# The sample's attention: from beside the output projection to between the steps of the prompt's attention

## Chip, core and metric

The kernel runs on one core of a Trainium2 chip. The metric is device time in microseconds (us) of one execution; less is better.

## What is computed

One inference step of a decoder layer, for a prompt of 2048 tokens and a sample group of 8 sequences with 8 new tokens each (64 tokens) over a cache of 2048 keys and values. The layer is h = x + W_o [A(n) | B(n)], y = h + W2 relu(RMSNorm(h) W1)^2, with n = RMSNorm(x), D = 1024. A is softmax attention, 8 heads of 64, over three strided key sets merged by their denominators; B is an RWKV-7 time mix. Cut to what matters here:

```
for w, d in ((128, 1), (512, 4), (2048, 16)):       # window, dilation
    s = q @ k[last w, every d].T * scale + bias     # masked to the band
    mx = max(s); e = exp(s - mx); dn = sum(e); o = e @ v
att = sum_b exp(mx_b - max mx) * o_b / sum_b exp(mx_b - max mx) * dn_b
h = x + concat(att, rwkv) @ w_out
```

It is evaluated once for the prompt (no cache) and once for the sample (keys and values from the cache and the 8 new ones).

## The kernel before

Everything is fp32; the large products are done with a high and a low part in three passes. The program is written tile by tile; a planner fixes the order of the instructions on every engine at compile time, by program order as priority and its own estimate of readiness. On the chip each engine, and SP's queue that issues nearly all transfers, goes through its list strictly in order.

**Stage 1** (until about 1208 us of the span): input projections and the RWKV scan. **Stage 2**, the prompt's attention: `attention(p, pump, ahead)` for four head pairs p. For each p it goes through three branches b; a branch has four groups, each with its own values tile `vt`. A step is: scores by two matmuls per block into a bank of `psc` (three banks, two used by a step; lines 1066 and 1067), bias and row minimum on VectorE (L1069), exp on ScalarE, transposes through `ppt` (two banks, L1084) and the product with the values into `ppo` (L1091). A step ends with `pump()`. There are 8 + 8 + 4 = 20 steps per p, 80 in all. `kq_load` fetches the next pair's queries and keys (12 transfers of 512 KB) during branch 1.

`merge(p)` is a generator that merges the three branches. It takes the statistics through a small DRAM tile (`wD`, L1166, back as `wrow`, L1169), then does 12 products (L1176) with a multiply on VectorE each, and stores `mixA` (L1181). `pump` advances the merge of the previous pair by two pieces; the merge of the last pair has nothing left to run beside and uses `psc`, the others `pax` (one bank).

**Stage 3**, the output projection: 8 chunks of 264 columns; for each of 8 output tiles 24 matmuls (L1431) into one of four `pwo` banks, 1536 in all, over panels `mr` of mixA and mixR (L1313) that are split into two parts first.

**The sample's attention** is `sample_attention(b, psa)`, a generator for one of the 8 sequences, with 8 pieces: three of scores (L1233, L1236: keys from the cache in tiles `kv` of 512 KB, L1231), one of exp and sums, three of transposes (L1269) and products with the values (L1277: values in `kv` tiles too, L1264) and one that transposes the result into `attS` (L1282). In the projection two pieces run after each output tile:

```
tt(h[:, o, c0:c0 + NC_], ps[:, :NC_], h[:, o, c0:c0 + NC_], ALU.add)
for _ in range(2):
    next(sample, None)
```

It has its own three PSUM banks (pool `psa`), four `kv` buffers in two pools, and one accumulation over all 11 value blocks. `attS` is needed by the last chunk only. The sample's bias (`sbias`, 32 small loads, L1341 to L1344), its queries and its new keys are loaded after the third pair's attention.

Of the kernel before, what the change touches and what calls it, by code (L numbers as in the profile page):

```python
# [17 lines left out]
P = 128  # L18
# [3 lines left out]
NS = 64  # L22
# [148 lines left out]
def _build(ctx, tc, nc, I, O, dbg, upto):  # L171
# [794 lines left out]
    ae = ph2.enter_context(pool(name="ae", bufs=1))  # L966
    ar = ph2.enter_context(pool(name="ar", bufs=1))

    kqb = ph3.enter_context(pool(name="kqb", bufs=6, side="right"))
# [38 lines left out]
    def bias_load(p, b):  # L1008
        bts = []
        for ty in range(2):  # L1010
            bt = ae.tile([P, 256], F32, name=f"bt{b}{ty}")
            nc.sync.dma_start(out=bt, in_=bass.AP(tensor=bvD.tensor, offset=bvD.offset + (2 * p + ty) * P * 1152 + b * 384 + 127, ap=[[1151, P], [1, 256]]))
            bts.append(bt)
        return bts
# [22 lines left out]
    def attention(p, pump, ahead):  # L1037
# [4 lines left out]
        for b in range(3):  # L1042
# [7 lines left out]
            for grp in range(4):  # L1050
                vp, vt = vt, next_v()
                o = ppo.tile([P, 512], F32, name="o")
                for t2 in range(0, 4, 2 if b < 2 else 4):
# [3 lines left out]
                    for ty in range(2):  # L1057
                        kst, klo, qst = K[ty]
                        ps = psc.tile([P, 512], F32, name="sc")
                        e = ae.tile([P, 512], F32, name="e", bufs=4)  # L1060
                        blocks = []
                        for x, i in enumerate(tl):
                            both = b < 2 and not (i == 0 if b == 0 else i < 4)
                            n = 256 if both else 128
                            c0 = x * w + w - n
                            PE.matmul(ps[:, c0:c0 + n], cols(qst, b, i, False), cols(kst, b, i, both), start=True, stop=False)  # L1066
                            PE.matmul(ps[:, c0:c0 + n], cols(qst, b, i, False), cols(klo, b, i, both), start=False, stop=True)  # L1067
                            nm, dn = st[:, 0, b, i // 4, ty, i % 4:i % 4 + 1], st[:, 1, b, i // 4, ty, i % 4:i % 4 + 1]
                            V.tensor_tensor_reduce(out=e[:, c0:c0 + n], in0=ps[:, c0:c0 + n], in1=bts[ty][:, 256 - n:256], scale=-1.0, scalar=3e38, op0=ALU.add, op1=ALU.min, accum_out=nm)  # L1069
# [33 lines left out]
    def merge(p, ob, st):  # L1103
# [46 lines left out]
        yield  # L1150
        dn = at.tile([P, P], F32, name="dn")
        dm = at.tile([P, P], F32, name="dm")
# [50 lines left out]

    kvs = []

    def kv_tile():

        kv_tile.n += 1
        pl, bufs = kvs[kv_tile.n % len(kvs)]
        return pl.tile([P, 1024], F32, name="kv", bufs=bufs)  # L1210

    kv_tile.n = -1

    def sample_attention(b, psa):
        pr = sat.tile([P, 136 + 520 + 1288], F32, name="pr")
# [11 lines left out]
        for k0, n, parts in runs:  # L1227
            ps = psa.tile([P, 512], F32, name="sc", tag="sp", bufs=2)
            for k1 in range(0, n, 256):
                kt = kv_tile().rearrange("p (q n) -> p q n", q=4)  # L1230
                nc.sync.dma_start(out=kt, in_=I["kc"][b, :, :, k0 + k1:k0 + k1 + 256].rearrange("p q n -> q p n"))  # L1231
                for p in range(4):
                    PE.matmul(ps[32 * p:32 * p + 32, k1:k1 + 256], qbd[:, b, p], kt[:, p], start=True, stop=True, tile_position=(0, 32 * p))  # L1233
            for p in range(4):
                if n == 256:
                    PE.matmul(ps[32 * p:32 * p + 32, 256:264], qbd[:, b, p], kSs[:, p, b * 8:b * 8 + 8], start=True, stop=True, tile_position=(0, 32 * p))  # L1236
            for x, dst, bias, s0, d0, w in parts + (new if n == 256 else ()):
# [13 lines left out]
        yield  # L1251
        o = psa.tile([P, 512], F32, name="ax", tag="ax")

        blocks = [(520 + i * P, P, 4 + i) for i in range(6)] + [(i * P, P, i) for i in range(4)] + [(512, 8, None)]
        for q0 in range(0, 11, 4):
            bl = blocks[q0:q0 + 4]
            vts = []
            for y in range(0, len(bl), 2):
# [6 lines left out]
                vts.append(vt)  # L1265
            pt = psa.tile([P, 512], F32, name="pt", tag="sp", bufs=2)
            pts = sat.tile([P, 512], F32, name="pts", bufs=2)
            for y, (c0, n, kb) in enumerate(bl):
# [3 lines left out]
            else:  # L1272
                V.tensor_copy(pts[:, :2 * P], pt[:, :2 * P])
                V.tensor_copy(pts[:8, 2 * P:3 * P], pt[:8, 2 * P:3 * P])
            for y, (c0, n, kb) in enumerate(bl):
                for p in range(4):
                    PE.matmul(o[32 * p:32 * p + 32, 0:P], pts[:n, y * P + 32 * p:y * P + 32 * p + 32], vts[y // 2][:n, y % 2, p * P:(p + 1) * P], start=(q0 == 0 and y == 0), stop=(kb is None), tile_position=(0, 32 * p))  # L1277
            yield
        os_ = sat.tile([P, P], F32, name="os", tag="pts", bufs=2)
        act(os_, o[:, :P], AF.Copy, scale=rd)  # L1280
        tp = psa.tile([P, 512], F32, name="tp", tag="sp", bufs=2)
        PE.transpose(tp[:, :P], os_, ident)  # L1282
# [4 lines left out]

    def sample_all(psa):
        for b in range(8):
            yield from sample_attention(b, psa)  # L1290

# [26 lines left out]

    rest = iter(())
    for p in range(4):  # L1320
        before = rest
        def pump():
            for _ in range(2):
                next(before, None)

        rest = attention(p, pump, ahead)
        for _ in before:
            pass
        if p == 2:
            kqa.close()  # L1330
            we = ph3.enter_context(pool(name="we", bufs=1, side="right"))
            sat = ph3.enter_context(pool(name="sat", bufs=1, side="right"))

    sbias = sat.tile([P, 136 + 520 + 1288], F32, name="sbias")
    sb1, sb4, sb16 = sbias[:, 0:136], sbias[:, 136:656], sbias[:, 656:]
    G.memset(sbias, 0.0)
    for h in range(8):
        r0 = 32 * (h // 2) + 8 * (h % 2)
        o0 = svD.offset + h * 8 * NSV + 7
        win = lambda b, c, n: bass.AP(tensor=svD.tensor, offset=o0 + b * 528 + c, ap=[[NSV - 1, 8], [1, n]])  # L1340
        nc.sync.dma_start(out=sb1[r0:r0 + 8], in_=win(0, 384, 136))  # L1341
        nc.sync.dma_start(out=sb4[r0:r0 + 8], in_=win(1, 0, 520))
        nc.sync.dma_start(out=sb16[r0:r0 + 8, :520], in_=win(2, 0, 520))
        nc.sync.dma_start(out=sb16[r0:r0 + 8, 520:].rearrange("i (m r) -> i m r", r=8), in_=bass.AP(tensor=svD.tensor, offset=o0 + 3 * 528, ap=[[NSV - 1, 8], [16, 96], [1, 8]]))  # L1344
    qSs = sat.tile([P, 4, NS], F32, name="qSs", tag="pts", bufs=2)
    nc.sync.dma_start(out=qSs, in_=qSD.rearrange("h p t -> p h t"))
    kSs = sat.tile([P, 4, NS], F32, name="kSs")
    nc.sync.dma_start(out=kSs, in_=kSD.rearrange("h p t -> p h t"))
    qbd = sat.tile([P, 8, 4, 32], F32, name="qbd")
    G.memset(qbd, 0.0)  # L1350
    for ty in range(2):
        rr = slice(ty * 64, ty * 64 + 64)
        for p in range(4):
            G.tensor_copy(qbd[rr, :, p, ty * 8:ty * 8 + 8], qSs[rr, p].rearrange("p (b i) -> p b i", i=8))
    attS = sat.tile([P, 4, NS], F32, name="attS")

    kvs.append((sat, 2))
    for k in (4, 5):
        wo_panel(we.tile([P, 2 * D], F32R, name=f"wo{k}"), k)
    mixed = {}  # L1360
    for k in range(4, 8):
        mixed[k, 0] = mix_panel(we, k, 0)
    for _ in rest:
        pass
    ph2.close()
# [42 lines left out]

    with pool(name="wo2", bufs=1) as wo2, pool(name="pwo", bufs=4, space=PSUM, side="right") as pwo, pool(name="psa", bufs=1, space=PSUM) as psa, pool(name="pst", bufs=1, space=PSUM) as pst:
        kvs.append((wo2, 2))  # L1410
        sample = sample_all(psa)
        for k in (6, 7, 0, 1, 2, 3):
# [4 lines left out]
        for c0 in range(0, NT, NC_):  # L1417
            if c0 + NC_ == NT:
                for _ in sample:
                    pass  # L1420
            nc.sync.dma_start(out=h[:, :, c0:c0 + NC_], in_=I["xh"][:, :, c0:c0 + NC_])  # L1421
# [3 lines left out]
            for o in range(KT):  # L1425
# [7 lines left out]
                tt(h[:, o, c0:c0 + NC_], ps[:, :NC_], h[:, o, c0:c0 + NC_], ALU.add)  # L1433
                for _ in range(2):
                    next(sample, None)
            while tile_ < 17 and ends[tile_] <= c0 + NC_ < NT:
# [110 lines left out]
```

## Time and profile before

| | |
|---|---|
| median of 3 runs | 3414.67 us (3407.58 to 3416.85) |
| the profiled execution's own time | 3415.77 us |
| its span | 3414.0 us |
| TensorE (PE) busy | 3209.2 us, 94% |
| PE weight loads (PEld) busy | 2791.4 us, 82% |
| VectorE (DVE) / ScalarE (ACT) / GpSimd (POOL) busy | 1713.4 / 1326.7 / 395.2 us |
| transfers | 364.73 MB, 107 GB/s over the span |

In the view of windows a row is a stretch from A to B us of the span, its length, the busy time of each engine with its instructions in brackets, the mean granted clock of TensorE as a share of 2.4 GHz (PEclk), the busy share of the 16 DMA engines, and GB/s. The chain is followed back from the last instruction; its rows have the start, the length and what ran. In the view of waits a row has who waited, for whom, the sum in us, how often, and the longest. In the timeline a row has the start, the length, the engine (SPq is SP's queue), the line and the instruction. In the view of groups a row has line, engine, operation, tiles, shapes, count, busy time and mean ns of one, and the idle time before.

### The profile page before, as it was taken

The numbers are of one execution on the slowest core, as the hardware profiler recorded it, in microseconds if no ns is written. First come the engines' busy times: TensorE is split into PE (matmuls) and PEld (weight loads), VectorE is DVE, ScalarE is ACT, GpSimd is POOL, SyncE is SP. The second block draws the span as 40 slices with busy tenths as digits, with TensorE's granted clock in tenths as the row PEclk, the third lists the DMA queues.
The fourth block names the chain that finished last, engine by engine and source line by source line (L and its number), as shares of the span: only waits on it lengthen the run. The fifth ranks groups of instructions, "written<-read, shape, count | busy, mean of one in ns | idle before, by whom it ended". The sixth has DMA issues, their size and how long they took to land.

```text
span 3414.0 us, 60201 instructions
## 1 busy us (share of the span) xinstructions
PE 3209.2 (94%) x23646; PEld 2791.4 (82%) x23646; DVE 1713.4 (50%) x3951; ACT 1326.7 (39%) x3209; POOL 395.2 (12%) x713
## 2 busy tenths in 40 slices
PE   5959999999999979989899999999999999999999
PEld 5836877786788857878688899999999988888887
DVE  4635676677677525546554643333333633333333
ACT  4435564565455536657322322222222322222221
POOL 1003243342354100111000000000000000000000
PEclk9979999999999989999899999999999999999999
DMA  5445464465355495333776111111111211111112
GB/s 165 136 141 161 131 191 139 119 174 145 112 146 153 131 212 113 94 87 99 261 244 206 44 47 44 47 44 44 44 46 44 97 49 49 48 50 47 50 47 74
DMA packets 336968, 364.73 MB, mean 107 GB/s; under 512 B 112907, under 2 KB 226374, under 8 KB 333612
## 3 DMA queue, kind: packets, MB, share of 16 engines
q1 hardware_dynamic: 336684, 360.88, 36.5%
q8 instruction: 186, 3.05, 0.4%
q14 instruction: 98, 0.80, 0.1%
HBM read 286.20 MB, written 79.30 MB: 107 GB/s over the span
## 4 chain that ended last, share of the span: by engine, by line
PE 59%; DMA 6%; DVE 2%; SPq 1%; issue 1%; ACT 1%; POOL 1%; DVEq 0%; ACTq 0%; POOLq 0%
PE pm L1505 21%; PE pm L1488 21%; PE pwo L1431 4%; PE o L1091 2%; PE sc L1066 2%; PE pt L1084 2%; PE sc L1067 2%; PE pj L789 1%; DMA kst<-khD 1%; DMA vt<-vD 1%; DMA kv<-in_kc 1%; DMA mr<-mixA 1%; SPq L1421 1%; PE sc L1233 0%; DMA wD<-wh 0%
## 5 line engine op out<-in xcount | busy, mean ns | idle before, releaser
L184 ACT ACTIVATE wh<-wr 128x512 fp32r<-128x512 f32 (+1 forms) x472 | 294.3, 624 | 1027.5 <-PE pm L1505 582.3
L181 DVE TENSOR_TENSOR wl<-wr,wh 128x512 fp32r<-128x512 f32 (+1 forms) x472 | 325.9, 692 | 425.0 <-ACT wh L184 410.7
L1488 PE MATMUL pm<-mml,wh 128*128 128x512 f32 (+2 forms) x1280 | 452.5, 354 | 3.3 <-DVE mml L181 3.3
L1488 PE MATMUL pm<-mmh,wh 128*128 128x512 f32 (+2 forms) x1280 | 454.8, 356 | 0.4 <-ACT mmh L184 0.4
L1488 PE MATMUL pm<-mmh,wl 128*128 128x512 f32 (+2 forms) x1280 | 452.8, 354 | 0.0
L1505 PE MATMUL pm<-fh,wh 128*128 128x512 f32 (+2 forms) x1280 | 450.5, 355 | 0.0
L1505 PE MATMUL pm<-fh,wl 128*128 128x512 f32 (+2 forms) x1280 | 449.6, 353 | 0.0
L1505 PE MATMUL pm<-fl,wh 128*128 128x512 f32 (+2 forms) x1280 | 448.4, 352 | 0.0
L181 DVE TENSOR_TENSOR h<-pm,h 128x364 f32<-128x364 f32 (+1 forms) x320 | 190.5, 598 | 423.9 <-PE pm L1505 423.7
L1488 PEld LDWEIGHTS pm<-mml,wh 128*128 128x128 f32 x1280 | 241.0, 188 | 27.4 <-DVE mml L181 5.9
L1488 PEld LDWEIGHTS pm<-mmh,wl 128*128 128x128 f32 x1280 | 241.9, 189 | 22.5
L1505 PEld LDWEIGHTS pm<-fh,wl 128*128 128x128 f32 x1280 | 240.7, 188 | 22.4
L1488 PEld LDWEIGHTS pm<-mmh,wh 128*128 128x128 f32 x1280 | 241.4, 189 | 19.9 <-ACT mmh L184 0.9
L1505 PEld LDWEIGHTS pm<-fl,wh 128*128 128x128 f32 x1280 | 240.0, 188 | 21.5
L1505 PEld LDWEIGHTS pm<-fh,wh 128*128 128x128 f32 x1280 | 240.3, 188 | 19.2
L789 PE MATMUL pj<-wh,nh 128*128 128x256 f32 (+1 forms) x816 | 237.3, 292 | 7.5 <-ACT qn L184 3.5
L789 PE MATMUL pj<-wh,nl 128*128 128x256 f32 (+1 forms) x816 | 236.2, 290 | 1.0 <-DVE nl L181 0.9
L330 PE MATMUL pj<-nh,wh 128*128 128x512 f32 (+3 forms) x600 | 222.7, 375 | 13.2 <-ACT nh L184 9.9
L789 PE MATMUL pj<-wl,nh 128*128 128x256 f32 (+1 forms) x816 | 234.6, 288 | 0.0
L330 PE MATMUL pj<-nl,wh 128*128 128x512 f32 (+3 forms) x600 | 221.6, 370 | 3.9 <-DVE nl L181 3.8
L330 PE MATMUL pj<-nh,wl 128*128 128x512 f32 (+3 forms) x600 | 217.5, 365 | 0.0
L184 ACT ACTIVATE e<-e,st 128x256 f32<-128x256 f32 (+1 forms) x384 | 174.3, 455 | 106.3 <-DVE st L1069 104.4
(295 smaller groups left out, 6105.3 us busy)
## 6 DMA issues: line engine op xcount, KB each, us to landing
wr<-in_w SPq DMA_DIRECT2D x256, 256.0 KB
wr<-in_wr SPq DMA_DIRECT2D x120, 256.0 KB
wr<-in_wq SPq DMA_DIRECT2D x96, 256.0 KB
kv<-in_kc SPq DMA_DIRECT2D x40, 512.0 KB
kv<-in_vc SPq DMA_DIRECT2D x40, 512.0 KB
xsD<-xst SPq DMA_DIRECT2D x56, 256.0 KB
xrkv<-xsD SPq DMA_DIRECT2D x32, 384.0 KB
vt<-vD SPq DMA_DIRECT2D x48, 256.0 KB
```

Of the source, the lines that this page charges most:

```text
L181: V.tensor_tensor(out, a, b, op)
L184: S.activation(out, in_, func, bias=bias, scale=scale, **kw)
L330: PE.matmul(ps[:m, :n], a[:, k, :m], b[h * 4 + k][:, c0:c0 + n], start=(h == 0 and i == 0), stop=(h == 1 and i == 11))
L789: PE.matmul(out, a[h * 2 + k][:, i * P:i * P + m], b[:, k, :], start=(h == 0 and q == 0 and i % 2 == 0), stop=(h == 3 and q == 5 and (i % ...
L1066: PE.matmul(ps[:, c0:c0 + n], cols(qst, b, i, False), cols(kst, b, i, both), start=True, stop=False)
L1067: PE.matmul(ps[:, c0:c0 + n], cols(qst, b, i, False), cols(klo, b, i, both), start=False, stop=True)
L1084: PE.transpose(pt[:, y * P:(y + 1) * P], e[:, c0:c0 + P], ident)
L1091: PE.matmul(o[ty * 64:ty * 64 + 64, (i % 4) * P:(i % 4 + 1) * P], kv[:, ty * 64:ty * 64 + 64], ptss[ty][:, y * P:(y + 1) * P], start=fst, ...
L1421: nc.sync.dma_start(out=h[:, :, c0:c0 + NC_], in_=I["xh"][:, :, c0:c0 + NC_])
L1431: PE.matmul(ps[:, :NC_], a[k][:, o * P:(o + 1) * P], b, start=(i == 0), stop=(i == 3 * KT - 1))
L1488: PE.matmul(ps[:, :n], a[:, k], b[:, hf * 4 + k, c0:c0 + n], start=(hf == 0 and i == 0), stop=(hf == 1 and i == 11))
L1505: PE.matmul(ps[:, :n], a[:, f], b[:, c0:c0 + n], start=(i == 0), stop=(i == 11))
```

## The change

The sample's pool, its bias, its new keys and `attS` are set up before the attention. `sample_attention` takes its banks from the prompt's pools (scores from `psc`, transposes from `ppt`, products from `pax`), its transposed weights from the prompt's `pts` buffers, and has two `kv` buffers. The queries are fetched per sequence, by two small loads, in place of one load and eight copies on GpSimd. The products with the values are accumulated over one piece at a time, and the three sums are added in SBUF. Every `pump()` advances the sample by one piece, so that its 64 pieces are used up after 64 of the 80 steps. To make room, the third branch's prompt bias is 128 columns wide and not 256, and `dn` shares a buffer with `nall`.

```diff
+    sat = ph3.enter_context(pool(name="sat", bufs=1, side="right"))
...
-            bt = ae.tile([P, 256], F32, name=f"bt{b}{ty}")
+            w = 256 if b < 2 else 128
+            bt = ae.tile([P, w], F32, name=f"bt{b}{ty}")
...
-        dn = at.tile([P, P], F32, name="dn")
+        dn = at.tile([P, P], F32, name="dn", tag="nall")
...
+    sbias = sat.tile([P, 136 + 520 + 1288], F32, name="sbias")
...
+    qbds = [sat.tile([P, 4, 32], F32, name=f"qbd{i}") for i in range(2)]
...
     def kv_tile():
-        kv_tile.n += 1
-        pl, bufs = kvs[kv_tile.n % len(kvs)]
-        return pl.tile([P, 1024], F32, name="kv", bufs=bufs)
...
+        return sat.tile([P, 1024], F32, name="kv", bufs=2)
...
+    def sample_attention(b):
+        qbd = qbds[b % 2]
+        for ty in range(2):
+            rr = slice(ty * 64, ty * 64 + 64)
+            nc.sync.dma_start(out=qbd[rr, :, ty * 8:ty * 8 + 8], in_=qSD[:, rr, b * 8:b * 8 + 8].rearrange("h p i -> p h i"))
...
-            ps = psa.tile([P, 512], F32, name="sc", tag="sp", bufs=2)
+            ps = psc.tile([P, 512], F32, name="sc")
...
-        o = psa.tile([P, 512], F32, name="ax", tag="ax")
+        os_ = sat.tile([P, P], F32, name="os")
...
-            pt = psa.tile([P, 512], F32, name="pt", tag="sp", bufs=2)
-            pts = sat.tile([P, 512], F32, name="pts", bufs=2)
+            pt = ppt.tile([P, 512], F32, name="pt")
+            pts = at.tile([P, 512], F32, name="pts", bufs=4)
...
+            o = pax.tile([P, 512], F32, name="ax")
...
+            if q0 == 0:
+                act(os_, o[:, :P], AF.Copy, scale=rd)
+            else:
+                stt(os_, o[:, :P], rd, os_, ALU.mult, ALU.add)
             yield
...
+    sample = sample_all()
...
         def pump():
             for _ in range(2):
                 next(before, None)
+            next(sample, None)
...
     for _ in rest:
+        pass
+    for _ in sample:
         pass
...
-    with pool(name="wo2", bufs=1) as wo2, pool(name="pwo", bufs=4, space=PSUM, side="right") as pwo, pool(name="psa", bufs=1, space=PSUM) as psa, pool(name="pst", bufs=1, space=PSUM) as pst:
-        kvs.append((wo2, 2))
-        sample = sample_all(psa)
+    with pool(name="wo2", bufs=1) as wo2, pool(name="pwo", bufs=4, space=PSUM, side="right") as pwo, pool(name="pst", bufs=1, space=PSUM) as pst:
...
-                for _ in range(2):
-                    next(sample, None)
```

## Rows read from the trace of the kernel before

**Rows 1.** The page, busy time and granted clock in 40 slices of 85 us.

```profile
PE   5959999999999979989899999999999999999999
PEclk9979999999999989999899999999999999999999
```

**Rows 2.** Windows, stretches of the attention and the projection.

```profile
core 0: us, PE busy (x) PEld busy (x) DVE busy (x) ACT busy (x) POOL busy (x), PEclk, DMA share, GB/s
1208.00:1318.00 110.00, 85.18 (x636) 69.26 (x635) 39.47 (x184) 57.07 (x193) 1.17 (x4) 0.85 0.65 151
...
1357.00:1370.00 13.00, 2.51 (x13) 2.15 (x13) 2.00 (x8) 0.83 (x5) 0.00 (x0) 0.61 0.72 154
...
1460.00:1470.00 10.00, 0.61 (x5) 0.37 (x4) 0.00 (x0) 1.63 (x6) 0.00 (x0) 0.78 0.76 171
...
1538.00:1639.00 101.00, 96.20 (x791) 79.64 (x789) 67.01 (x257) 73.75 (x247) 17.82 (x29) 0.99 0.37 99
1639.00:1672.00 33.00, 23.02 (x203) 10.19 (x205) 25.57 (x68) 7.09 (x15) 0.00 (x0) 0.60 0.86 286
...
1720.00:1870.00 150.00, 146.83 (x1692) 131.26 (x1693) 73.63 (x253) 39.41 (x90) 2.18 (x1) 1.00 0.70 225
1870.00:1925.00 55.00, 54.03 (x455) 53.15 (x446) 20.94 (x60) 10.76 (x27) 0.00 (x0) 1.00 0.13 35
```

**Rows 3.** Chain of waits, start of the attention.

```profile
1199.95 16.76 DMA kst<-khD
...
1253.02 17.88 DMA vt<-vD
```

**Rows 4.** Waits of PE's matmuls, 1208 to 1640 us.

```profile
PE ax L1176 <- DMA wrow<-wD: 21.3, 2, 10.8
...
PE o L1091 <- DMA vt<-vD: 4.4, 1, 4.4
...
PE sc L1066 <- DVE st L1069: 0.5, 2, 0.3
```

**Rows 5.** Windows, the projection's matmuls alone (L1431).

```profile
1720.00:1870.00 150.00, 112.78 (x830) 103.55 (x830) 1.00 0.70 225
1870.00:1925.00 55.00, 52.12 (x418) 51.21 (x418) 1.00 0.13 35
```

**Rows 6.** Windows, the sample's products with values alone (L1277).

```profile
1720.00:1870.00 150.00, 17.10 (x517) 13.15 (x520) 1.00 0.70 225
```

**Rows 7.** Groups by form, 1640 to 1930 us, the sample's three largest on PE.

```profile
L1233 PE MATMUL sc<-kv,qbd 128*32 128x256 f32 x316 | 27.0, 440 | 7.2 <-DMA kv<-in_kc 7.2
...
L1277 PE MATMUL ax<-kv,pts 128*32 128x128 f32 x640 | 22.2, 283 | 1.4 <-DMA kv<-in_vc 1.4
...
L1269 PE MATMUL pt<-ident,pr 128*128 128x128 f32 x80 | 14.1, 297 | 3.4 <-ACT pr L184 3.4
```

**Rows 8.** Timeline, the last pair's merge.

```profile
1648.84 1.35 SPq L1166 DMA_DIRECT2D wD<-wh  x4
...
1657.37 0.96 PE L1176 MATMUL sc<-wrow,wsel 128*128 128x512 f32 x3
...
1672.22 0.59 PE L1431 MATMUL pwo<-mh,wo 128*128 128x264 f32 x1
```

**Rows 9.** Timeline, the third pair's merge.

```profile
1560.07 1.78 SPq L1166 DMA_DIRECT2D wD<-wh  x4
...
1567.64 0.43 PE L1176 MATMUL ax<-wrow,wsel 128*128 128x512 f32 x1
```

**Rows 10.** Timeline of SP's queue, first and last of the 32 loads of the sample's bias.

```profile
1538.77 0.30 SPq L1341 DMA_DIRECT2D sbias<-svD  x1
...
1558.37 0.30 SPq L1344 DMA_DIRECT2D sbias<-svD  x1
```

**Rows 11.** Waits of SP's queue, 1640 to 1930 us.

```profile
SPq L1264 <- PE ax L1277: 24.0, 6, 9.5
...
SPq L1231 <- PE ax L1277: 12.4, 10, 2.3
```

More of the change, by code (lines that the diff above doesn't have):

```diff
@@ L1010, in bias_load @@
         for ty in range(2):
-            bt = ae.tile([P, 256], F32, name=f"bt{b}{ty}")
-            nc.sync.dma_start(out=bt, in_=bass.AP(tensor=bvD.tensor, offset=bvD.offset + (2 * p + ty) * P * 1152 + b * 384 + 127, ap=[[1151, P], [1, 256]]))
+            w = 256 if b < 2 else 128
+            bt = ae.tile([P, w], F32, name=f"bt{b}{ty}")
+            nc.sync.dma_start(out=bt, in_=bass.AP(tensor=bvD.tensor, offset=bvD.offset + (2 * p + ty) * P * 1152 + b * 384 + 383 - w, ap=[[1151, P], [1, w]]))
             bts.append(bt)
@@ L1068, in attention @@
                             nm, dn = st[:, 0, b, i // 4, ty, i % 4:i % 4 + 1], st[:, 1, b, i // 4, ty, i % 4:i % 4 + 1]
-                            V.tensor_tensor_reduce(out=e[:, c0:c0 + n], in0=ps[:, c0:c0 + n], in1=bts[ty][:, 256 - n:256], scale=-1.0, scalar=3e38, op0=ALU.add, op1=ALU.min, accum_out=nm)
+                            V.tensor_tensor_reduce(out=e[:, c0:c0 + n], in0=ps[:, c0:c0 + n], in1=bts[ty][:, bts[ty].shape[1] - n:], scale=-1.0, scalar=3e38, op0=ALU.add, op1=ALU.min, accum_out=nm)
                             act(e[:, c0:c0 + n], e[:, c0:c0 + n], AF.Exp, bias=nm, scale=-1.0, accum_out=dn)
@@ L1201, in _build @@
     mv2 = at.tile([P, 2, 2, 4, 4, 8], F32, name="mv2")
-    kvs = []
-    def kv_tile():
-        kv_tile.n += 1
-        pl, bufs = kvs[kv_tile.n % len(kvs)]
-        return pl.tile([P, 1024], F32, name="kv", bufs=bufs)
-    kv_tile.n = -1
-    def sample_attention(b, psa):
+    sbias = sat.tile([P, 136 + 520 + 1288], F32, name="sbias")
+    sb1, sb4, sb16 = sbias[:, 0:136], sbias[:, 136:656], sbias[:, 656:]
+    G.memset(sbias, 0.0)
+    for h in range(8):
+        r0 = 32 * (h // 2) + 8 * (h % 2)
+        o0 = svD.offset + h * 8 * NSV + 7
+        win = lambda b, c, n: bass.AP(tensor=svD.tensor, offset=o0 + b * 528 + c, ap=[[NSV - 1, 8], [1, n]])
+        nc.sync.dma_start(out=sb1[r0:r0 + 8], in_=win(0, 384, 136))
+        nc.sync.dma_start(out=sb4[r0:r0 + 8], in_=win(1, 0, 520))
+        nc.sync.dma_start(out=sb16[r0:r0 + 8, :520], in_=win(2, 0, 520))
+        nc.sync.dma_start(out=sb16[r0:r0 + 8, 520:].rearrange("i (m r) -> i m r", r=8), in_=bass.AP(tensor=svD.tensor, offset=o0 + 3 * 528, ap=[[NSV - 1, 8], [16, 96], [1, 8]]))
+    kSs = sat.tile([P, 4, NS], F32, name="kSs")
+    nc.sync.dma_start(out=kSs, in_=kSD.rearrange("h p t -> p h t"))
+    qbds = [sat.tile([P, 4, 32], F32, name=f"qbd{i}") for i in range(2)]
+    for t in qbds:
+        G.memset(t, 0.0)
+    attS = sat.tile([P, 4, NS], F32, name="attS")
+    def kv_tile():
+        return sat.tile([P, 1024], F32, name="kv", bufs=2)
[4 more added lines that the diff above has]
+            nc.sync.dma_start(out=qbd[rr, :, ty * 8:ty * 8 + 8], in_=qSD[:, rr, b * 8:b * 8 + 8].rearrange("h p i -> p h i"))
         pr = sat.tile([P, 136 + 520 + 1288], F32, name="pr")
@@ L1232, in sample_attention @@
                 for p in range(4):
-                    PE.matmul(ps[32 * p:32 * p + 32, k1:k1 + 256], qbd[:, b, p], kt[:, p], start=True, stop=True, tile_position=(0, 32 * p))
+                    PE.matmul(ps[32 * p:32 * p + 32, k1:k1 + 256], qbd[:, p], kt[:, p], start=True, stop=True, tile_position=(0, 32 * p))
             for p in range(4):
                 if n == 256:
-                    PE.matmul(ps[32 * p:32 * p + 32, 256:264], qbd[:, b, p], kSs[:, p, b * 8:b * 8 + 8], start=True, stop=True, tile_position=(0, 32 * p))
+                    PE.matmul(ps[32 * p:32 * p + 32, 256:264], qbd[:, p], kSs[:, p, b * 8:b * 8 + 8], start=True, stop=True, tile_position=(0, 32 * p))
             for x, dst, bias, s0, d0, w in parts + (new if n == 256 else ()):
@@ L1274, in sample_attention @@
                 V.tensor_copy(pts[:8, 2 * P:3 * P], pt[:8, 2 * P:3 * P])
+            o = pax.tile([P, 512], F32, name="ax")
             for y, (c0, n, kb) in enumerate(bl):
                 for p in range(4):
-                    PE.matmul(o[32 * p:32 * p + 32, 0:P], pts[:n, y * P + 32 * p:y * P + 32 * p + 32], vts[y // 2][:n, y % 2, p * P:(p + 1) * P], start=(q0 == 0 and y == 0), stop=(kb is None), tile_position=(0, 32 * p))
+                    PE.matmul(o[32 * p:32 * p + 32, 0:P], pts[:n, y * P + 32 * p:y * P + 32 * p + 32], vts[y // 2][:n, y % 2, p * P:(p + 1) * P], start=(y == 0), stop=(y == len(bl) - 1), tile_position=(0, 32 * p))
+            if q0 == 0:
+                act(os_, o[:, :P], AF.Copy, scale=rd)
+            else:
+                stt(os_, o[:, :P], rd, os_, ALU.mult, ALU.add)
             yield
-        os_ = sat.tile([P, P], F32, name="os", tag="pts", bufs=2)
-        act(os_, o[:, :P], AF.Copy, scale=rd)
-        tp = psa.tile([P, 512], F32, name="tp", tag="sp", bufs=2)
+        tp = ppt.tile([P, 512], F32, name="pt")
         PE.transpose(tp[:, :P], os_, ident)
@@ L1286, in sample_attention, with sample_all @@
         yield
-    def sample_all(psa):
+    def sample_all():
         for b in range(8):
-            yield from sample_attention(b, psa)
+            yield from sample_attention(b)
     NT = T + NS
@@ L1331, in _build @@
             we = ph3.enter_context(pool(name="we", bufs=1, side="right"))
[L1332 to L1357, printed above, removed]
     for k in (4, 5):
@@ L1417, in _build @@
         for c0 in range(0, NT, NC_):
-            if c0 + NC_ == NT:
-                for _ in sample:
-                    pass
             nc.sync.dma_start(out=h[:, :, c0:c0 + NC_], in_=I["xh"][:, :, c0:c0 + NC_])
```

## The prediction

> **What bounds the kernel now.** I read the slices of the page first, then windows by stage, then the chain and the waits inside the two stages that the change touches. The slices show PE at 9 tenths nearly everywhere, with dips in slices 15, 18 and 20 (from 1195, 1451 and 1622 us), and the granted clock is lower in the first and last of these [rows 1]: the gain, if any, must come from PE's holes, because the PE work of the sample is moved and not removed. The windows place them [rows 2]. The projection has hardly any: 54.03 busy of 55 us in its last two chunks, 146.83 of 150 where the sample runs beside it. The attention has three large ones: 25 us of the first 110, and two gaps of 13 and 10 us. Between them it is nearly as full as the projection, 96.20 of 101 us. The 33 us after the last step are a fourth weak stretch, with a mean clock of 0.60, between the two levels of 1.2 and 2.4 GHz.
>
> What makes the holes is told by the chain and the waits. At the start it is transfers: the keys (16.76 us) and later a values tile (17.88 us) stand in the chain [rows 3]. The two later gaps are PE standing before a merge product, 21.3 us in two waits, until the merge's round trip through DRAM is back [rows 4]; DMA is 72 and 76% busy then [rows 2]. Those holes wait for transfers. They can take the sample's matmuls only if its keys are there at that moment and if the planner has put those matmuls ahead of the waiting one.
>
> **What the projection gets back.** From the first projection matmul at 1672.2 us [rows 8] to 1925 are 253 us. The two last chunks, almost without sample, give the rate: 55 us for 418 matmuls, 0.132 us each, small waits included [rows 5]. 1536 matmuls take 202 us. Gain 51 us.
>
> Before it, the merge of the last pair takes 33 us [rows 2], and the sample's first sequence and a half runs in its waits. Without it the merge does not stand in line with the sample on VectorE and in the DMA queue: the trip from the store to the first product took 8.5 us with the sample [rows 8] and 7.6 us earlier [rows 9], and the 12 products with their multiplies then ran to 1672, 14.9 us, with the sample's reductions in between. I take 26 for 33, a gain of 7 (ends 0 and 12). But PE now idles for most of these 26 us and starts the projection at the lower clock; the stretch that has 0.60 now stands for what that does, and I take 3 us of loss. Together the second half gains 51 + 7 - 3 = 55 us.
>
> **What the attention pays on PE.** In 1720 to 1870 the projection's 830 matmuls are worth 830 x 0.132 = 109 us; the other 41 us are the sample's [rows 5], and 517 of its 704 products with values lie there, 73% [rows 6]. So the whole sample costs PE 41 / 0.73 = 56 us. The groups bound it from above: the three largest are busy for 27.0 + 22.2 + 14.1 = 63 us [rows 7], ends that overlap included. Below, the price is what does not fit into holes. By PE's busy time a steady stretch has 4.8 us free of 101 [rows 2], which over the 300 us from 1318 to 1639 without the gaps is 14 us. I take 56 - 14 = 42 us; ends 0 and 63.
>
> By the weight load's busy time there is more room: 79.64 of 101 us against 53.15 of 55 in the projection [rows 2]. The Trainium skill (Perfetto Trace Analysis, section Identifying the Most-Contended Engine) says that matmul busy time does not measure how close TensorE is to its limit, since matmuls are pipelined, and that the weight load's busy share does. By that rule the 42 us would be near 3, and the sum a gain. I stay with the busy row because the free weight-load time lies in short pauses of a step that waits for exp and for transposed blocks, and the sample brings its own switches between kinds of matmul; but this is the first rival.
>
> **What the attention pays elsewhere.** Four edits have no row of their own before. *The start*: 32 bias loads, the new keys and the queries now stand on SP before the second values tile. On SP the bias loads took from 1538.8 to 1558.7, with others between [rows 10]; some 12 us are their own issue time, and the start is held by transfers already [rows 3]. Ends 0 and 20; I take 8. *The merge gaps*: 80 `kv` loads, 41 MB less the small ones, are added to a stage whose two gaps wait for a round trip in a queue that is over 70% busy. Ends -15 (the sample fills them) and +20; I take 8. *Late keys and values*: with four buffers PE waited 7.2 us for keys and 1.4 for values [rows 7]; now there are two, and a piece of scores uses both. Ends 0 and 30; I take 8, the row itself. *The banks*: a score piece holds one of three `psc` banks, so a step that needs two cannot start ahead; with three banks PE waited 0.5 us for the reductions [rows 4]. Ends 0 and 20; I take 5. VectorE and ScalarE have the time: 67 and 74 of 101 us [rows 2]. The narrower bias, the shared `dn` (written after the last read of `nall`) and the sums in SBUF lie beside PE and cost nothing while it is the bound; the eight dropped copies on GpSimd, idle there, give nothing.
>
> **The sum.** 42 + 8 + 8 + 8 + 5 = 71 us paid against 55 gained: +16 us on the profiled execution's own 3415.8, 3432. That execution lies 1.1 us above the median, so 3431.
>
> **Rivals.** *The holes take it (faster).* The steps of the attention wait on each other's exp; another, independent chain fills the pauses, as the weight loads suggest: (0.966 - 0.789) x 300 = 53 us of room for 56 us of work. The PE term falls to 3, the sum to 3 + 8 + 8 + 8 + 5 - 55 = -23: 3392; with the gaps filled as well, 3370. For it speaks that the planner may take any ready matmul; against it that PE already shows 96 of 101.
>
> *SP's queue blocks (much slower).* A `kv` load must wait until PE has used one of the two buffers, and behind it in the same queue stand the values tiles, the next pair's keys and the merge's round trip. With four buffers SP waited 24.0 and 12.4 us for the value products alone [rows 11]. If these waits double and fall on loads that PE needs, 36 us come on top of the sum and about 10 from longer merge gaps: 3477. It decides from the point where a values tile lands after its group has begun, which the start already shows once, by 4.4 us [rows 4].
>
> *It slips back.* If keys come too slowly, the planner pushes the pieces to the end of the attention, and they run in the last merge's waits as they do now. The attention pays less, the projection gains less: about 3416.
>
> **How the numbers follow.** The forecast 0.48, the holes 0.27, the blocked queue 0.17, the slip 0.08. A measurement here tells 0.3%, 10 us, from no change. Faster by more: the holes nearly whole and a little of the forecast, 0.28. Within: the slip and the low part of the forecast, 0.21. Slower: 0.51. Both signs are likely, so the forecast's own range is 3412 to 3452; the range for 8 in 10 is 3388 to 3470, which leaves out the best of the holes (all gaps filled) and the worst of the queue.
>
> **What would show it.** Right: the projection from its first matmul to the MLP near 202 us with no sample in it; the last merge near 26 us with PE mostly idle; the attention longer by about 70 us, of which PE's busy time takes some 56 and its waits for transfers the rest. The first step wrong: the attention grows by under 30 us with PE's weight load near 90%. The transfers wrong: waits of PE for `kv`, `vt` and `wrow` under 20 us in all, or far over 50. The projection wrong: it is still over 220 us without the sample.

## The result, and the profile after

The changed kernel takes 3516.73 us (median of 4 runs, 3513.72 to 3518.99) against 3411.34 for the kernel before on the same chips: ratio 1.0307, 95% interval 1.0287 to 1.0327, so 105 us slower. Forecast were 16 us slower, at most 54. The profiled execution has a span of 3511.6 us, 98 more than before.

Windows of the changed kernel, with the columns of [rows 2]: the first 110 us of the attention, most of its third pair, the last merge, the projection, and the whole attention.

```profile
1208.00:1318.00 110.00, 48.54 (x402) 34.73 (x404) 25.19 (x107) 28.09 (x91) 0.00 (x0) 0.67 0.76 178
...
1538.00:1640.00 102.00, 76.92 (x635) 53.87 (x636) 50.65 (x195) 43.60 (x139) 11.00 (x10) 0.82 0.67 172
...
1794.00:1826.00 32.00, 14.41 (x60) 9.65 (x61) 23.50 (x48) 8.35 (x17) 0.00 (x0) 0.63 0.40 122
...
1875.00:2022.00 147.00, 146.09 (x1194) 145.34 (x1193) 56.37 (x152) 30.75 (x71) 1.81 (x1) 1.00 0.16 44
1208.00:1800.00 592.00, 472.38 (x4171) 364.84 (x4171) 286.18 (x1190) 295.71 (x986) 43.35 (x56) 0.86 0.58 152
```

The projection is what was forecast: PE busy 146.09 of 147 us. The attention is not. PE was busy for 85 us of the first 110 before, now for 49; the stretch from 1538 us, in which it had 96.20 of 101 us [rows 2], now has 76.92 of 102 (it was the last pair, without next keys to load; now it is the third, with them). The granted clock is 0.86 over the whole, with stretches nearer to the lower level where PE stands still.

Who PE's matmuls waited for from 1208 to 1805 us (waits; sum, times, longest), beside [rows 4]:

```profile
PE sc L1252 <- DMA kv<-in_kc: 66.2, 14, 19.6
PE ax L1297 <- DMA kv<-in_vc: 15.2, 4, 7.6
...
PE o L1093 <- DVE pts L991: 2.2, 5, 0.7
```

The waits for the merge's trip (21.3 us) and for a values tile (4.4 us) are gone, and the sample's cached keys and values are waited for 81 us, mostly in a few long waits. The timeline shows one of them, at the start of the third pair:

```profile
1540.87 0.54 SPq L1005 DMA_DIRECT2D kst<-khD  x1
...
1552.25 2.83 SPq L1005 DMA_DIRECT2D klo<-klD  x2
...
1559.54 3.80 SPq L1250 DMA_DIRECT2D kv<-in_kc  x2
...
1573.90 1.08 PE L1252 MATMUL sc<-kv,qbd 128*32 128x256 f32 x8 [16.56 <-DMA kv<-in_kc]
```

and the windows of that stretch show what the DMA engines did meanwhile:

```profile
1540.00:1560.00 20.00, 13.05 (x112) 8.15 (x112) 9.76 (x33) 7.36 (x19) 0.81 (x2) 0.83 1.06 237
1560.00:1574.00 14.00, 0.10 (x4) 0.13 (x8) 0.00 (x0) 0.00 (x0) 0.00 (x0) 0.51 0.95 223
```

`kq_load` stands in branch 1, but SP issues its twelve transfers (6 MB) around the pair's first step, from 1532 us, the last at about 1555; the cached keys are asked for at 1559.54 and arrive 14 us later. DMA is full all the time, PE stands for 16.56 us with 0.10 us of work in the last 14, at a clock of 0.51.

By pairs, from the first score matmul of a pair to that of the next (the last one to the last product with values), then the last merge and the projection's matmuls, in us, from the traces of both and of the experiments below:

| | pair 1 | pair 2 | pair 3 | pair 4 | merge | projection |
|---|---|---|---|---|---|---|
| before | 116.2 | 104.2 | 105.2 | 103.2 | 33.2 | 250.2 |
| changed | 181.4 | 149.6 | 148.2 | 112.0 | 24.6 | 198.8 |
| e1, no cache loads | 154.1 | 118.4 | 124.7 | 107.8 | 24.7 | 197.8 |
| e2, from the second pair | 119.9 | 143.8 | 151.3 | 143.9 | 30.5 | 198.5 |
| e9, before, no next keys | 117.5 | 91.9 | 92.9 | 99.4 | 36.2 | 247.4 |
| e10, changed, no next keys | 147.9 | 132.0 | 125.2 | 106.6 | 28.5 | 196.6 |
| e11, as e10, six buffers | 133.1 | 122.6 | 123.6 | 110.6 | 26.2 | 195.2 |
| e12, before, keys after the trip | 112.4 | 91.9 | 94.9 | 99.3 | 36.5 | 247.9 |
| e13, changed, keys spread | 164.7 | 132.5 | 136.1 | 108.4 | 28.5 | 194.4 |
| e14, changed, no loads, no next keys | 141.3 | 115.0 | 124.7 | 107.8 | 25.6 | 197.3 |

The change gives 60 us back in the last two columns and pays 162 in the pairs; the start comes 5 us earlier.

### The profile page after: what moved, and what is told of

It reads as the page before. It is cut to its first block, busy times and chain, and to the rows that moved or that the text cites. A ratio compares the mean times of both kernels' runs of the same rounds, so it can differ in the third digit from the quotient of the medians.

```text
span 3511.6 us, 60284 instructions
## 1 busy us (share of the span) xinstructions
PE 3243.4 (92%) x23646; PEld 2807.1 (80%) x23646; DVE 1723.0 (49%) x3967; ACT 1327.8 (38%) x3209; POOL 393.8 (11%) x706
## 4 chain that ended last, share of the span: by engine, by line
PE 77%; DMA 11%; DVE 5%; POOL 2%; ACT 2%; SPq 2%; issue 2%; DVEq 0%; ACTq 0%; POOLq 0%
PE pm L1481 21%; PE pm L1498 21%; PE pj L330 8%; PE pwo L1426 5%; PE pj L789 5%; PE o L1093 3%; PE sc L1068 2%; PE pt L1086 2%; PE sc L1069 2%; DMA kv<-in_kc 2%; DMA kst<-khD 1%; POOL itmp L566 1%; DMA klo<-klD 1%; POOL xt L567 1%; PE pu L655 1%
## 5 line engine op out<-in xcount | busy, mean ns | idle before, releaser
L1481 PEld LDWEIGHTS pm<-mmh,wl 128*128 128x128 f32 x1280 | 242.9, 190 | 22.5
L1071 DVE CUSTOM_DVE_ANT_0 e<-sc,bt 128x256 f32<-128x256 f32 (+1 forms) x384 | 133.4, 362 | 187.8 <-PE sc L1069 134.5
```

The source lines that it names most:

```text
L1481: PE.matmul(ps[:, :n], a[:, k], b[:, hf * 4 + k, c0:c0 + n], start=(hf == 0 and i == 0), stop=(hf == 1 and i == 11))
```

## Experiments

Diffs are against the changed kernel, where not said otherwise. Times are medians with the ratio to the kernel before, run on the same chip.

**e1, e4: the price of the loads and the price of the sample.**

```diff
# e1: one tile of keys and one of values are loaded once
-                kt = kv_tile().rearrange("p (q n) -> p q n", q=4)
-                nc.sync.dma_start(out=kt, in_=I["kc"][b, :, :, k0 + k1:k0 + k1 + 256].rearrange("p q n -> q p n"))
+                kt = kvc[0].rearrange("p (q n) -> p q n", q=4)
...
# e4, against the kernel before
-                for _ in range(2):
-                    next(sample, None)
```

> The changed kernel with the 80 loads of cached keys and values left out: one tile of each is loaded once and used by every piece, so the sample's output is that of wrong keys, and all its engine work stays. Theory (late transfers): the attention grew by 158 us, of which PE's own work is some 56; the other 100 are pieces that wait for keys and values that arrive late (81 us of PE waits) and the low clock after them. Without the loads the attention takes about 490 us in place of 590 and the kernel 3415 to 3435. Rival (engines and banks): the growth is the sample's PE, ScalarE and VectorE work in shared PSUM banks; then the time stays over 3490.

> The kernel before with the sample's attention left out (its result is set to zero). All theories: the attention is as before, 431 us; the projection's matmuls take about 202 us from first to last in place of 253, the last merge about 26 us, and the kernel about 3357. If the projection stays over 215 us, the sample was cheaper beside it than was reckoned, and the gain side of the forecast is wrong.

e1 took 3431.72 us (1.0055, 1.0036 to 1.0074), e4 3350.80 (0.9817, 0.9797 to 0.9836). So 85 of the 105 us hang on the 80 loads (with them go eight small ones of the new values). And the sample beside the projection cost 62 us (3412.87 - 3350.80), which is what the move can win at most; 198.3 us of projection and 21.4 of merge in e4 agree with the gain side of the forecast. Without its cache loads the moved sample is still 19 us slower than before.

**e2: starting with the second pair** (`if p: next(sample, None)` in the pump).

> The changed kernel with the sample's pieces starting with the second pair's steps in place of the first's (the small loads before the attention stay). Theory (the start is special: the first transfers of keys stand behind the 6 MB of the second pair): the first pair took 181 us with and 116 us without the sample, of which 42 us are waits for keys; it falls to about 130 us, the last pair pays about 30 to 45 us for its pieces, and the kernel takes 3490 to 3505. Rival (a piece costs the same everywhere): no change, 3510 to 3520.

3490.37 us (1.0230, 1.0207 to 1.0254). The first pair falls to 119.9 us, 4 more than before: about that is the price of the small loads at the start (in e4 and e12, which like the kernel before have none there, it takes 113.9 and 112.4). Each pair with 20 pieces costs 40 to 46 us more than before, the last one too, which has no next keys to load; the sample's start is 20 us dearer than that (what it is: e16).

**e3: another queue** (the three loads of cached data on `nc.gpsimd`).

> The changed kernel with the loads of cached keys and values issued on GpSimd's queue and not on SP's. Theory A (order in the queue: keys stand behind the next pair's 6 MB and the values tiles): with a queue of their own they come in time, PE's waits for them fall from 81 us to under 40, and the kernel takes 3460 or less. Theory B (two buffers: a load is issued only when PE has used the tile before, whatever the queue): the waits stay between 60 and 100 us, and the kernel takes 3500 to 3530.

3522.70 us (1.0313, 1.0288 to 1.0339), no gain. PE's waits for cached data are still 35.4 and 16.7 us, with 18.4 more for the queries:

```profile
PE sc L1252 <- DMA kv<-in_kc: 35.4, 12, 8.1
PE sc L1252 <- DMA qbd<-qSD: 18.4, 1, 18.4
PE ax L1297 <- DMA kv<-in_vc: 16.7, 5, 5.6
```

So for the cached data the order in SP's queue is not it (the queries had stayed there; e16 comes back to them). That left buffers, bytes, or DMA engines that are full whatever queue asks. The trace of e3 speaks for the last, since for this queue the view of DMA has the median time from issue to landing (last column), here of the cached keys from 1420 to 1535 us, without next keys, and then from 1541 to 1570 us, beside them:

```profile
kv<-in_kc POOLq DMA_DIRECT2D x10, 512.0 KB, 4.3
kv<-in_kc POOLq DMA_DIRECT2D x4, 512.0 KB, 15.7
```

With a queue of its own a load of the same size takes more than three times as long beside the next pair's keys.

**e5 to e8: bytes and buffers.**

```diff
# e5: two fixed tiles, of which each load renews a part
-                nc.sync.dma_start(out=kt, in_=I["kc"][b, :, :, k0 + k1:k0 + k1 + 256].rearrange("p q n -> q p n"))
+                nc.sync.dma_start(out=kt[:, :, :32], in_=I["kc"][b, :, :, k0 + k1:k0 + k1 + 32].rearrange("p q n -> q p n"))
...
# e6; e7 has the second and third change alone (pts in all its places)
-        return sat.tile([P, 1024], F32, name="kv", bufs=2)
+        return sat.tile([P, 1024], F32, name="kv", bufs=3)
-                    e = ae.tile([P, 512], F32, name="e", bufs=4)
+                    e = ae.tile([P, 512], F32, name="e", bufs=3)
...
-                    pts = at.tile([P, 512], F32, name="pts", bufs=4)
+                    pts = at.tile([P, 512], F32, name="pts", bufs=3)
...
# e8
-        return sat.tile([P, 1024], F32, name="kv", bufs=2)
+        return sat.tile([P, 512], F32, name="kv", bufs=4)
```

> The changed kernel with all 80 cache loads and both buffers kept, but each load brings only a small part of its tile (64 KB in place of 512; the rest of the two tiles is loaded once and stays, so the sample's output is that of wrong keys and values). The loads cost 85 us (3517 against 3432 without them). Theory A (round trip: a load is issued only after PE has let go of the buffer, and PE then stands through the queue and the landing, whatever its size): most of it stays, 3480 to 3515. Theory B (bytes: the transfer of 512 KB, 2 us at full rate and longer beside other transfers, is what comes late): most of it goes, 3430 to 3455.

> The changed kernel with three buffers for cached keys and values in place of two; to make room, the prompt's e and pts have three buffers in place of four. To be read against the next run, which has the same e and pts. Theory A (round trip with two buffers): the next piece's first tile is on its way while PE works; 20 to 40 us less than the next run. Theory B (bytes): the DMA engines were at 62% in the second and third pair, so an earlier issue helps too, but the bursts of the next pair's keys stay in front: 5 to 20 us less.

> The control for the run before: the changed kernel with three buffers for e and pts and two for cached keys and values. PE's steps hang on e and pts little: 3515 to 3535.

> The changed kernel with cache tiles of half the size and four buffers, the same 8 KB per partition and the same bytes, in 160 loads. Theory A (round trip): SP issues twice as many loads and each still waits for its buffer; the matmuls can begin at the first half: 3500 to 3530. Theory B (bytes): PE can begin after 256 KB and gives back after it, so half of a tile's transfer is hidden: 3475 to 3500.

e5 took 3491.43 us (1.0229, 1.0214 to 1.0245), e6 3505.14 (1.0270, 1.0253 to 1.0287), e7 3524.37 (1.0329, 1.0313 to 1.0344), e8 3513.54 (1.0294, 1.0279 to 1.0310). An eighth of the bytes takes 25 of the 85 us away; a third buffer 19 (e6 against e7); half tiles 3, within the spread of the runs. Theory A seemed to hold. But the waits of e5 say what is left there, and its timeline where two of the longer ones are:

```profile
PE sc L1259 <- DMA kvc<-in_kc: 51.3, 10, 21.6
PE ax L1304 <- DMA kvc<-in_vc: 13.0, 2, 11.5
```

```profile
1277.95 1.08 PE L1259 MATMUL sc<-kvc,qbd 128*32 128x256 f32 x8 [5.90 <-DMA kvc<-in_kc]
...
1295.55 1.08 PE L1259 MATMUL sc<-kvc,qbd 128*32 128x256 f32 x8 [6.71 <-DMA kvc<-in_kc]
```

The wait of 21.6 us is the first one of the attention, of which e16 tells. The other nine, 30 us together, are for loads of 64 KB, which had an eighth of the bytes. Six of them, 28.7 us, end between 1277 and 1296 or between 1536 and 1568 us, beside the twelve transfers of a next pair's keys (issued from 1259 to 1278 and from 1526 to 1552 us) or up to 18 us behind them, where the DMA share is 0.99 (1270 to 1296) and 0.94 (1540 to 1570). From 1300 to 1390 us, where it is 0.20, PE is busy for 87.40 of 90 us. (e5 has smaller pieces in the same number, so it does not tell bytes from the cost of a piece.)

**e9 to e11: without the next pairs' keys.** `kq_load` returns the first pair's tiles for all pairs; in e11 cached data use six tiles of the pool that this leaves free.

> The kernel before with the loads of queries and keys of the second to fourth pair left out (all pairs use the first pair's, so the attention's output is wrong; its work is the same). It is the control for the next two runs. The two gaps of 13 and 10 us, in which PE waits for the merge's round trip behind these loads, should go, and some of the start: 3380 to 3395.

> The changed kernel with the same loads left out, 18 MB of the attention's traffic. Theory A (a tile is asked for only when PE has let go of its buffer, and PE then stands through the trip): the distance to the run before stays 90 us or more. Theory C (bursts: the long waits for cached keys, 22 and 11 us even with small loads, are those behind the next pair's 6 MB): the distance falls from 105 to about 50 us.

> As the run before, with six buffers for cached keys and values during the first three pairs (in the room that the left-out keys give). Theory A: with the next two or three pieces on their way the loads cost little; 30 us or more below the run before, near 45 us above the control. Theory C: the bursts are gone already, so the buffers give under 15 us.

e9 3407.02 us (0.9983, 0.9973 to 0.9992), e10 3460.61 (1.0144, 1.0127 to 1.0160), e11 3449.25 (1.0104, 1.0089 to 1.0119). The distance from e10 to its control e9 is 54 us: with the bursts, half of the loss goes. Six buffers give 11 more; e11 begins its attention 13 us later than e10, so its pairs alone are 22 us shorter. e9 itself gained less than expected. Its attention begins at 1227 and not at 1210 us, because SP issues the first keys at 1214.56 and not at 1196.17; that its one set of keys lies in the other pool may be why, which was not tried. e10 has the same edit and begins at 1229. The second and third pair of e9 are 12 us shorter each, about the two gaps of [rows 2].

**e13: the burst spread in the changed kernel.** Each tile of the next pair's keys waits for one group of the second or third branch:

```diff
+                gate = yield
+                t = kq.tile([P, T], F32R, name=f"{nm}{ty}", tag="kq")
+                G.tensor_copy(t[:, 0:1], gate)
...
+                if p < 3 and b and (b == 1 or grp < 2):
+                    spread.send(st[:, 0, b, grp, 0, 0:1])
```

> The changed kernel, correct, with the next pair's queries and keys loaded one tile (two transfers of 512 KB) after each group of the second branch and two groups of the third, each held until VectorE has done that group's minimum, in place of twelve transfers in a burst. Theory C (the cached keys are late because they stand behind the burst): most of the 50 us that the bursts cost comes back, 3455 to 3480. Theory A (round trip with two buffers) or a limit of the DMA engines' rate: the same bytes and the same buffers, 3500 or more.

3471.46 us (1.0170, 1.0155 to 1.0185): 45 us back with the same bytes and buffers. PE waits 27.3 and 14.1 us for cached data, in place of 66.2 and 15.2, at a higher mean DMA share:

```profile
1390.00:1535.00 145.00, 132.36 (x1303) 101.90 (x1300) 85.82 (x360) 82.00 (x273) 14.83 (x22) 0.92 0.69 187
```

**e14, e15: the engines' price.** e14 is e1 without the next pairs' keys; e15 is e9 with `psc` of two banks.

> The changed kernel without the 80 cache loads and without the next pairs' keys (both as in the runs before, wrong output): the sample's engine work alone in an attention without gaps. Its distance to the kernel before without next keys (3407) is the engines' price, less the 55 us that the projection gives back, plus the start. If the sample costs PE what it costs beside the projection (56 us): 3407 to 3420. If it costs more among the prompt's steps, about 30 us per 20 pieces as the pairs suggest: 3430 to 3445, hardly below the run with six buffers (3449).

> The kernel before without next keys (3407) and with two psc banks for scores in place of three in the whole attention: the price of a score bank. If the sample's extra cost among the prompt's steps comes from the bank that its score pieces hold (24 of 64 pieces), a bank that is missing in all 80 steps costs 30 us or more. If not: under 10 us, and the extra cost is elsewhere (order on VectorE and ScalarE, transposes).

e14 3432.57 us (1.0056, 1.0041 to 1.0071), e15 3426.35 (1.0038, 1.0026 to 1.0049; its runs spread from 3417 to 3432). By pairs e14 pays 87 us over e9, 10 of them a wait for the first queries (e16): 77 us for engine work that the prediction put at 56 beside the projection, and that cost 62 there by e4, its loads and waits included. A score bank less in all 80 steps costs 19 us, between the two ends expected; the sample's score pieces hold one in 24 of 80 steps, so by an estimate from these counts (19 x 24 / 80) it explains some 6 of the 15 to 21 us between. The windows of the second pair, e9 first (1345 to 1436) and then e14 (1360 to 1480, with the last 8 us of the first pair):

```profile
1345.00:1436.00 91.00, 90.49 (x746) 76.29 (x745) 55.94 (x235) 64.55 (x225) 12.91 (x16) 1.00 0.20 59
```

```profile
1360.00:1480.00 120.00, 117.32 (x1167) 94.68 (x1168) 75.08 (x324) 77.05 (x265) 12.98 (x16) 0.99 0.17 46
```

PE is busy for 90.49 of 91 and 117.32 of 120 us. The weight load's share falls from 76.29 of 91 to 94.68 of 120, 84 to 79%, when the sample comes in: its short pauses are not filled, more are added. What makes the rest, 9 to 15 us (switches between kinds of matmul, order on VectorE and ScalarE) was not tried.

**e16, e17: the first wait.** In the first pair PE waits 19.6 us for the first cached keys, in e13 19.4, in e5 21.6, in e1 22.5 for the first queries. SP's timeline of the changed kernel shows the sample's bias loads ahead of both, 32 issues in 16 us:

```profile
1227.80 0.31 SPq L1213 DMA_DIRECT2D sbias<-svD  x1
...
1243.04 0.47 SPq L1216 DMA_DIRECT2D sbias<-svD  x1
...
1245.54 1.31 SPq L1233 DMA_DIRECT2D qbd<-qSD  x2
1246.89 1.15 SPq L1250 DMA_DIRECT2D kv<-in_kc  x2
```

```diff
# e16; e17 has the same in e13; so for all four loads of each of the eight heads
-        nc.sync.dma_start(out=sb1[r0:r0 + 8], in_=win(0, 384, 136))
+        G.dma_start(out=sb1[r0:r0 + 8], in_=win(0, 384, 136))
```

> The changed kernel with the 32 loads of the sample's bias on GpSimd's queue; all else as it was. Theory A, the loads hold SP's queue: PE's first wait for cached keys (19.6 us) falls to 5 us or less, the first pair to about 166 us, the kernel to about 3502. Theory B, the second pair's burst and full DMA engines make that wait: it stays at 15 to 20 us and the kernel within 4 us of 3517. If GpSimd issues the 32 loads more slowly than SP, the first bias comes late instead, and VectorE, not PE, waits for it: some of the gain is lost.

> The kernel with spread keys (3471 us) with the same 32 loads on GpSimd's queue. Theory A: its wait of 19.4 us at the start goes, about 3456. Theory B: the wait was there even with the burst spread, so the burst can hardly be it; if it stays, something else is late (the first queries or GpSimd's own issue), 3468 to 3475.

e16 took 3524.11 us (1.0337, 1.0322 to 1.0353), 7 more than the changed kernel; e17 3466.07 (1.0164, 1.0139 to 1.0189), 5 less than e13, with intervals that overlap. Theory A is wrong on the time, and the shorter wait bears it out only in part. The wait falls to 7.74 and 8.36 us (theory A: 5 or less), but in e16 because PE comes to it 13 us later: the first matmul with cached keys starts at 1252.27 us, and at 1251.24 in the changed kernel. There SP's queue does hold the load: PE waits from 1231.6 us, the load is issued only at 1246.89, behind the 32, and is used 4.4 us later. Without the 32 on SP it is issued only 3 us earlier, at 1243.67, and takes 8.6 us, so what the queue gave back was lost elsewhere. In e16 PE also waits 16.4 us for the first pair's own queries, where it waited 9.8, and a later wait for cached keys, behind the second pair's burst, is 26.58 us long:

```profile
1227.92 0.44 PE L1068 MATMUL sc<-kst,qst 128*128 128x128 f32 x1 [14.99 <-DMA qst<-qlD]
...
1243.67 1.84 SPq L1250 DMA_DIRECT2D kv<-in_kc  x2
...
1252.27 1.08 PE L1252 MATMUL sc<-kv,qbd 128*32 128x256 f32 x8 [7.74 <-DMA kv<-in_kc]
...
1289.39 1.08 PE L1252 MATMUL sc<-kv,qbd 128*32 128x256 f32 x8 [26.58 <-DMA kv<-in_kc]
```

The windows of 1200 to 1250 us, the changed kernel first and then e16, show what else changed. The 32 loads lie in both. On SP they stand alone: from 1228 to 1244 us the DMA share is 0.43. On GpSimd's queue, which is free from 1208 us, they run beside the first pair's keys, and the DMA engines are full throughout.

```profile
1200.00:1250.00 50.00, 10.59 (x58) 7.89 (x56) 1.93 (x9) 4.18 (x12) 2.01 (x3) 0.59 0.79 174
```

```profile
1200.00:1250.00 50.00, 12.61 (x80) 10.24 (x78) 2.02 (x9) 4.29 (x12) 22.31 (x35) 0.61 1.09 190
```

**e12: a version that beats both.** Against the kernel before: the third and fourth pair's keys are held until the merge's trip is back.

```diff
+            if p > 1:
+                for t in (kst, klo, qst):
+                    G.tensor_copy(t[:, 0:1], wrow[:, 0, 0:1].bitcast(F32))
             for dst, src, r0 in ((kst, khD, 0), (qst, qhD, 0), (kst, khD, 64), (qst, qlD, 64), (klo, klD, 0), (klo, klD, 64)):
```

> The kernel before, correct, with the loads of the third and fourth pair's queries and keys held until the previous merge's trip through DRAM is back (one column of each of their tiles is written by GpSimd from what the trip brings). If PE's gaps of 13 and 10 us come from that trip standing behind these loads, both go: 15 to 23 us less, 3390 to 3398. If the loads then come too late for the next pair, the gaps move to the pair's start, and nothing is gained.

3386.07 us (0.9920, 0.9905 to 0.9935), 27 us less than the kernel before, of which the second and third pair give 23 (table). SP's part of the timeline shows the trip, 3.6 us from the store to the fetch, ahead of the burst; before, the stores stretched over 6.6 us and the fetch came at 1365.30:

```profile
1344.43 1.33 SPq L1169 DMA_DIRECT2D wD<-wh  x4
...
1347.98 0.68 SPq L1172 DMA_DIRECT2D wrow<-wD  x2
...
1351.62 0.48 SPq L1007 DMA_DIRECT2D kst<-khD  x1
```

The second pair has no gap (windows), and the next pair's keys are in time:

```profile
1323.00:1430.00 107.00, 106.43 (x886) 88.75 (x885) 67.33 (x287) 77.92 (x272) 15.24 (x26) 1.00 0.48 116
```

## Why the prediction was wrong

The direction was right, the size far off: 105 us against 16, outside the range. Step by step:

- **The reading of [rows 1]**: slice 20 is no dip of PE, which has 9 tenths there; only its clock is lower. Nothing in the sum hangs on it.
- **The projection's 51 us and the merge's 7**: right. The matmuls go from 250.2 to 198.8 us, the merge from 33.2 to 24.6. The 3 us for the lower clock were not measured alone.
- **Late keys and values, 8 us, "the row itself", and the merge gaps, 8 us**: this is the step that failed. The row was taken in the projection, where there were four buffers and no next pair's keys to load; its upper end, 30, was too low as well. The merge's trip, for which the second term stood, is not waited for any more. e1 puts the loads at 85 us. e10 with e14 says that without bursts they cost 28 (3460.61 - 3432.57), so 57 come from meeting the bursts, and e13 takes 45 of these back in the kernel as it is. The prediction's own sign, waits for `kv`, `vt` and `wrow` far over 50 us, came true with 81. The prediction had the two pieces side by side: DMA at 72 and 76% with PE standing before a trip [rows 2, 4], and a new consumer that needs 80 loads in 64 steps, up to 1 MB in one. The kernel before, in windows over its whole attention and ahead of those two gaps:

```profile
1208.00:1640.00 432.00, 380.38 (x3002) 316.87 (x3004) 226.16 (x956) 270.89 (x930) 46.49 (x66) 0.92 0.49 117
1330.00:1357.00 27.00, 27.00 (x246) 21.63 (x243) 20.02 (x81) 23.23 (x76) 0.00 (x0) 1.00 1.04 210
1430.00:1460.00 30.00, 29.93 (x268) 23.83 (x266) 22.09 (x93) 25.39 (x87) 1.54 (x4) 1.00 0.99 205
```

  The bursts fill DMA for some 30 us each, and PE is not held up there because nothing it needs is loaded then. The prediction counted the burst as a risk for the merge only, and not for the cached keys, which PE now needs at the same place of its fixed order.
- **PE's 42 us**: mis-sized too, 77 by e14 against e9; after the loads this is the second largest part of the miss. The 56 us came out of the projection's stretch; among the prompt's steps a piece costs more, for reasons that stay partly open (e15), and the 14 us of holes took nothing visible.
- **The start, 8 us**: the small loads cost about 4 (e2). But e2 had put what waits for them a pair later. Where PE needs the first queries and keys at once, it waits some 20 us behind the 32 bias loads on SP: the upper end of the term, which was 20. On another queue (e16, e17) the first cached keys are used hardly earlier, at 1252 and 1253 us, against 1251 in the changed kernel and 1256 in e13.
- **The banks, 5 us**: about 6, an estimate from e15; it is part of the 77.
- **The rival "the holes take it"** and the rule beside it: fell. The prompt's steps left the weight load some 18% below its share beside the projection [rows 2], and with the sample in, the measured share went down, not up. The Trainium skill's rule (Perfetto Trace Analysis, section Identifying the Most-Contended Engine) judges how near TensorE is to its limit; here its free share, 16% in e9, did not take in the sample's work, and the measurement decides.
- **The rival "SP's queue blocks"** had the largest size and the wrong place: what was late were not the values tiles or keys behind the `kv` loads (PE's wait for `vt` is gone) but the `kv` loads behind the keys, and not by the queue but in DMA engines that were full: on a queue of their own they land after 15.7 us beside the bursts and after 4.3 without (e3). Only at the start does SP's queue hold PE, for most of the first 19.6 us (e16).

## What to carry to other kernels

When work with its own loads is moved into another stage, look at that stage's transfers in windows of some 30 us and not on the mean: 0.49 over the attention hid bursts near 1.0, and PE, in a fixed order, stood behind each. A burst that is needed only with the next pair can be tied to a later event, for which a few bytes written by an idle engine are enough; that alone was worth 45 us in the changed kernel and 27 in the one before. And a price measured beside one kind of work (56 us) need not hold beside another (77).

## Not expected of the hardware

Two sets of loads got a queue of their own, and neither gained. The cached data on GpSimd's queue were still waited for 52 us (e3, 3522.70 against 3516.73 us). And when the 32 loads of the sample's bias, 0.5 MB in all (64 rows of 1944 elements of 4 bytes), moved beside the keys (e16), the DMA engines' busy share over 50 us rose from 0.79 to 1.09, and the rate only from 174 to 190 GB/s. The view of DMA by queue (packets, MB, share of the 16 engines), 1200 to 1250 us, first SP's queue in the changed kernel, then SP's and GpSimd's in e16:

```profile
q1 hardware_dynamic: 12724, 8.67, 79.1%
```

```profile
q1 hardware_dynamic: 6347, 8.95, 97.8%
q0 software_dynamic: 1104, 0.50, 11.0%
```

The small loads themselves take 11.0%. The larger part is SP's own transfers, which take 97.8% for 8.95 MB, where they took 79.1% for 8.67 MB with the 32 loads among them. What makes them longer was not tried.
